# Accumulators of one PSUM bank in place of halves of a bank pair: a hybrid HGRN2 / Mamba-2 layer on one core

## The chip, the core and the metric

The kernel runs on one core of a Trainium2 chip, as one program. A core has TensorE (PE, matmuls), VectorE (DVE), ScalarE (ACT), GpSimd (POOL) and DMA queues, which SyncE (SP) issues here. Matmuls write into PSUM, of which the kernel uses eight banks of 512 float32 a partition; DVE and ACT read it. Each engine works off its own queue in order and waits on semaphores for the others. The metric is the time of one execution in microseconds on the device.

## The reference, cut to what matters

One inference step of one layer over T = 1048 tokens: 16 meta tokens, 1024 of a prompt, 8 single-token samples. Everything is float32.

```
h += 0.5 * SwiGLU_1(rmsnorm(h))                      D = 1024, hidden 2816
u  = rmsnorm(h) @ w_in                               q, f, i, g | z | x, B, C | dt
HGRN2, 4 heads of 128:  S_t = diag(f_t) S_{t-1} + k_t v_t^T,  o_t = S_t^T q_t,  k = 1 - f
        o = rmsnorm per head(o) * silu(g)
Mamba-2, 8 heads of 64: causal conv(4) + SiLU on x, B, C
        h_t = exp(dt_t A) h_{t-1} + dt_t x_t B_t^T,  y_t = h_t C_t + D x_t
        y = grouped rmsnorm(y * silu(z))
h += concat(o, y) @ w_out
h += 0.5 * SwiGLU_2(rmsnorm(h));  final rmsnorm of the outputs
```

The last states of both recurrences and of the convolution are outputs too.

## The kernel before

**Matmuls.** A float32 product is made of three matmuls on operands split into a high part (rounded by a copy on ACT) and a low part (a subtraction on DVE): `mm3`, lines 143 (high x high), 144 (high x low) and 145 (low x high). A *unit* is one accumulator's chain of such triples. Its result is read out of PSUM by an *evacuation* on ACT or DVE.

**Tokens.** The FFNs and out_proj work on quarters of Q = 262 tokens, two of them (c = 0, 1, or a half) at a time; the mixer's projections on chunks of 350, 350 and 348.

**PSUM.** Two pools share the eight banks: `mis`, four tiles of one bank for transposes, norms and scans (`psm()`), and `acc`, two tiles of two banks each, for the accumulators. `psum2()` hands out a whole tile, `psum()` the first half of a new tile and, at the next call, its second half. A tile's place comes free when all that was done with the tile is done.

**FFN** (`ffn`, line 691; hand-ordered). Both FFNs use products of a seven-multiplication scheme, numbered p. In `pair`, the gate and up products of one block of 128 hidden columns, p runs over 1, 6, 2, 5, 7, 3, 4; products 2, 3 and 4 add onto the accumulators of 1, 5 and 7. Except in the first pair of each FFN a unit pair (c = 0 and c = 1) shares one `psum2()` tile, which one instruction then reads whole. In the first pair (`first1`, `first2`) the operands are still being made (lines 281 to 298: scaling and high parts on ACT, sums and low parts on DVE), and each c has its own `psum()`; the accumulator of p = 7 and 4 is a `psm()`. There the copy of p = 1 is line 451, the reads of p = 6, 5, 3 are lines 453, 458 and 462. `down` runs p over 1, 5, 6, 7, 3, 4, 2; each p has four column groups j of 2 x 33 matmuls. The first six products use `psum2()`, the last (p = 2) one `psum()` per c and j: four units with c = 0, then four with c = 1. Line 647 is the evacuation (multiply by 0.5 and add to h) on DVE; lines 618 and 623 split the weights, 557 and 561 the hidden operand. What follows an FFN (`after1`: the next norm, lines 200 to 211, and the mixer's operand, lines 247 to 250; `after3`: the final norm and the stores) is hung between the steps of the last product. `Steps` holds the order: `before(i, fn)` puts work ahead of step i, and inside `manual_schedule` PE, DVE, ACT and SP keep that order.

**Mixer** (not ordered by hand: the tile library's planner plays the program through at build and fixes each engine's order from it). `proj` makes 24 matmuls of 350 columns for each chunk into a `psum()`; evacuations are on ACT: line 990 (x, B, C), 1308 (raw q or f), 1299 (v), 1289 (q), 1293 and 1294 (f), 1302 (g), 1246 (z). Between them stand `ssm_scan` (lines 1091 to 1158) and, for each of four heads, `hgrn_scan` (lines 1337 to 1505, among them the level products 1398 and 1407 that wait for DVE's line 1422), all in `mis` tiles. `K.weights` loads and splits weights (lines 137 and 138).

**out_proj** (planned too): four calls of 16 units of 12 matmuls, for half 0 and half 1 of the tokens and two halves of the contraction; each unit has a `psum()`, and line 1529 on DVE adds it to h. Behind half 0 the second FFN's `first2` begins on ACT and DVE.

**The end.** `LastFinal` normalizes the last three token tiles: `second` transposes into one `psum2()` and one `psm()` (line 1579) and ACT sums squares (line 1582); `third` does the last block.

## Time and profile before

| | us |
|---|---|
| median of 3 runs | 2083.57 (2081.5 to 2094.95) |
| profiled execution, its own time | 2081.47 |
| its span, first to last instruction | 2079.8 |
| PE busy | 1970.9 |
| DVE busy | 1474.5 |
| ACT busy | 825.2 |

The profile is of one execution. Times in it count from the span's start. In a row of the timeline stand start, duration, engine, line of the kernel, operation, output <- input and in brackets how long the engine stood before it and what ended that. A row of the waits gives who waited for whom, the sum, the number of times and the longest. Matmuls overlap: a duration of 0.28 us belongs to one every 0.12.

### The profile page before, as it was taken

The page shows a single profiled execution, that of the slowest core. Times are in us where ns is not written, and L with a number is a line of the kernel's source. Part 1 is how long each engine was busy: PE and PEld are TensorE (multiplying, and loading weights), DVE is VectorE, ACT ScalarE, POOL GpSimd, SP SyncE. Part 2 cuts the span into 40 slices and gives each one's busy share as a digit, 9 for nine tenths or more (in the row PEclk, how much of TensorE's full clock was granted, in tenths as well). Part 3 has the DMA queues.
Part 4 walks back from the last instruction along what each step waited for, and adds up shares of the span by engine and source line. Part 5 has one row for each costly group of instructions (what it writes and reads, how often), then busy time and mean ns, then how long its engine had stood idle before and what let it go on. Part 6 is the DMA issues. An engine that isn't in the chain of part 4 may idle for free.

```text
span 2079.8 us, 40798 instructions
## 1 busy us (share of the span) xinstructions
PE 1970.9 (95%) x16647; PEld 1915.7 (92%) x16647; DVE 1474.5 (71%) x2465; ACT 825.2 (40%) x1540; POOL 156.2 (8%) x197
## 2 busy tenths in 40 slices
PE   5899999999999899889989989989999999999996
PEld 5899999999999889888988878889999999999996
DVE  6777777777788676596455346777777777768973
ACT  7522222223534543574443344652222222354352
POOL 3000000000003210332011101210000000000000
PEclk8999999999999999999999999999999999999999
DMA  6223242335967621362022153222333242587851
GB/s 196 87 80 108 78 124 83 103 91 180 313 201 228 181 58 33 101 181 80 33 83 74 31 176 124 78 74 86 110 92 108 78 124 78 155 241 239 266 174 60
DMA packets 325042, 259.32 MB, mean 125 GB/s; under 512 B 17712, under 2 KB 301104, under 8 KB 324848
## 3 DMA queue, kind: packets, MB, share of 16 engines
q1 hardware_dynamic: 324616, 256.68, 40.7%
q8 instruction: 131, 2.15, 0.4%
q14 instruction: 55, 0.45, 0.1%
q0 software_dynamic: 224, 0.04, 0.0%
q10 hardware_dynamic: 16, 0.00, 0.0%
HBM read 191.26 MB, written 65.47 MB: 123 GB/s over the span
## 4 chain that ended last, share of the span: by engine, by line
PE 77%; DVE 10%; ACT 5%; DMA 4%; issue 3%; SPq 1%; POOL 0%; DVEq 0%; ACTq 0%; POOLq 0%
PE acc L143 24%; PE acc L145 23%; PE acc L144 23%; DMA r<-in_w_in_dram 1%; DVE u L561 1%; DVE ws L623 1%; DVE s L647 1%; DMA r<-in_w_ffn_up_dram 1%; DVE s L590 1%; DVE ws L138 1%; DMA r<-in_w_ffn_down_dram 1%; DVE u L287 0%; DVE ws L368 0%; PE mis L1449 0%; DVE r L613 0%
## 5 line engine op out<-in xcount | busy, mean ns | idle before, releaser
L143 PE MATMUL acc<-u,ws 128*128 128x262 f32 (+2 forms) x4504 | 1320.5, 294 | 39.3 <-ACT t L451 9.9
L145 PE MATMUL acc<-u,ws 128*128 128x262 f32 (+2 forms) x4504 | 1310.6, 291 | 0.6 <-DVE ws L368 0.5
L144 PE MATMUL acc<-u,ws 128*128 128x262 f32 (+2 forms) x4504 | 1309.1, 291 | 1.5 <-DVE u L561 1.5
L143 PEld LDWEIGHTS acc<-u,ws 128*128 128x128 f32 x4504 | 853.1, 190 | 54.4 <-ACT t L451 10.7
L144 PEld LDWEIGHTS acc<-u,ws 128*128 128x128 f32 x4504 | 857.8, 190 | 3.3 <-DVE u L561 1.9
L145 PEld LDWEIGHTS acc<-u,ws 128*128 128x128 f32 x4504 | 852.7, 189 | 2.6 <-DVE ws L368 1.1
L368 DVE TENSOR_TENSOR ws<-r,ws 128x512 fp32r<-128x512 f32 x308 | 211.7, 688 | 76.7 <-ACT ws L364 76.7
L364 ACT CAST ws<-r 128x512 fp32r<-128x512 f32 x308 | 173.2, 615 | 4.7 <-PE acc L145 3.1
L464 ACT ACTIVATE t<-t 128x524 f32<-128x524 f32 (+1 forms) x46 | 28.7, 623 | 305.4 <-DVE t L446 305.4
L360 DVE TENSOR_TENSOR r<-r,r 128x512 f32<-128x512 f32 x176 | 121.9, 695 | 11.7 <-DMA r<-in_w_ffn_up_dram 10.1
L204 POOL TENSOR_TENSOR t<-t,t 128x262 f32<-128x262 f32 x56 | 55.7, 1010 | 782.6 <-PE acc L145 626.6
L456 ACT ACTIVATE t<-t 128x524 f32<-128x524 f32 (+1 forms) x46 | 28.7, 624 | 215.3 <-DVE t L446 215.3
L561 DVE TENSOR_TENSOR u<-u,u 128x1048 fp32r<-128x1048 f32 (+1 forms) x84 | 97.8, 1166 | 8.8 <-ACT u L557 8.4
L138 DVE TENSOR_TENSOR ws<-r,ws 128x512 fp32r<-128x512 f32 x88 | 65.1, 753 | 48.0 <-ACT ws L137 47.9
L446 DVE TENSOR_TENSOR t<-t,u 128x524 f32<-128x524 f32 (+1 forms) x138 | 89.8, 679 | 3.3
L557 ACT CAST u<-u 128x1048 fp32r<-128x1048 f32 (+1 forms) x84 | 83.2, 993 | 1.3 <-DMA u<-hd 1.3
L647 DVE SCALAR_TENSOR_TENSOR s<-acc,s 128x524 f32<-128x524 f32 (+1 forms) x88 | 55.7, 648 | 38.1 <-PE acc L145 37.5
L137 ACT CAST ws<-r 128x512 fp32r<-128x512 f32 x88 | 53.9, 617 | 71.8 <-PE acc L145 42.4
L618 ACT CAST ws<-u 128x512 fp32r<-128x512 f32 (+1 forms) x72 | 42.1, 585 | 100.8 <-DVE u L613 95.0
L623 DVE TENSOR_TENSOR ws<-r,ws 128x512 fp32r<-128x512 f32 (+1 forms) x84 | 57.6, 697 | 32.6 <-ACT ws L618 32.5
L618 ACT CAST ws<-r 128x512 fp32r<-128x512 f32 (+1 forms) x84 | 47.4, 581 | 71.6 <-DVE r L613 41.0
L446 DVE TENSOR_TENSOR t<-acc,u 128x524 f32<-128x524 f32 (+1 forms) x46 | 31.3, 680 | 60.6 <-PE acc L145 60.6
(388 smaller groups left out, 1908.1 us busy)
## 6 DMA issues: line engine op xcount, KB each, us to landing
hd<-s SPq DMA_DIRECT2D x170, 262.0 KB
u<-hd SPq DMA_DIRECT2D x64, 524.0 KB
r<-in_w_ffn_down_dram SPq DMA_DIRECT2D x128, 256.0 KB
r<-in_w_ffn_gate_dram SPq DMA_DIRECT2D x88, 256.0 KB
r<-in_w_ffn_up_dram SPq DMA_DIRECT2D x88, 256.0 KB
r<-in_w_in_dram SPq DMA_DIRECT2D x56, 256.0 KB
r<-in_w_ffn_down_dram SPq DMA_DIRECT2D x64, 192.0 KB
u<-hd SPq DMA_DIRECT2D x28, 393.0 KB
```

The source lines that it names most:

```text
L138: self.nc.vector.tensor_sub(lo, src, hi.bitcast(F32))
L143: mm(ps, whi, xhi, start=first, stop=False, skip_group_check=more)
L144: mm(ps, whi, xlo, start=False, stop=False, skip_group_check=more)
L145: mm(ps, wlo, xhi, start=False, stop=last, skip_group_check=more)
L360: self.K.nc.vector.tensor_tensor(self.raw[p], self.raw[x], self.raw[y], op)
L364: self.K.nc.scalar.copy(self.w[p][:, : self.n * P], self.raw[p])
L368: self.K.nc.vector.tensor_sub(t[:, 512 : 512 + w], self.raw[p], t[:, :w].bitcast(F32))
L446: nc.vector.tensor_mul(t, t if src is None else src, spread.lanes(i, cs))
L557: K.nc.scalar.copy(hi, lo.bitcast(F32))
L561: K.nc.vector.tensor_sub(lo, lo.bitcast(F32), hi.bitcast(F32))
L618: nc.scalar.copy(w[p, j, g][:, : n * P], src)
L623: nc.vector.tensor_sub(t[:, 512 : 512 + n * P], box[0], t[:, : n * P].bitcast(F32))
```

## The change

Every accumulator that is read by itself becomes a tile of one bank. The pool `acc` now has either four tiles of one bank (`banks(1)`) or two tiles of two (`banks(2)`), on the same four banks. `banks(n)` closes the pool and opens the other. It is opened with four; at step 14 of each FFN, the first behind the first pair, it becomes two pairs; ahead of the last down product four again, which stay for the mixer, out_proj and the second FFN's first pair, or for the end. `psum()` no longer splits a pair, and `second` takes two tiles. No arithmetic, transfer or evacuation is changed.

```diff
-        self.acc = ent(tc.tile_pool(name="acc", bufs=2, space=PSUM))
         self.mis = ent(tc.tile_pool(name="mis", bufs=4, space=PSUM))
...
-        self.half = None
+        self.banks_ = ent(ExitStack())
+        self.banks(1)
+
+    def banks(self, n):
+
+        self.banks_.close()
+        self.acc = self.banks_.enter_context(self.tc.tile_pool(name="acc", bufs=4 // n, space=PSUM))
+        self.pairs = n == 2
...
     def psum2(self):
-        self.half = None
+        assert self.pairs
         return self.acc.tile([P, 2, 512], F32, tag="acc", name=self.uid("acc"))
 
     def psum(self):
-
-        if self.half is None:
-            t = self.psum2()
-            self.half = t
-            return t[:, 0]
-        t, self.half = self.half, None
-        return t[:, 1]
+        assert not self.pairs
+        return self.acc.tile([P, 512], F32, tag="acc", name=self.uid("acc"))
...
         else:
+            S.before(b, lambda: K.banks(1))
             then = after(S, h, b - 48 + 24, b + 12, b + 24)
...
         S = Steps()
+        S.before(14, lambda: K.banks(2))
         hidden = Hidden(K)
...
-        two = K.psum2()
-        self.ps = [two[:, 0], two[:, 1], K.psm()]
+        self.ps = [K.psum(), K.psum(), K.psm()]
```

## Prediction

> **What bounds the kernel now.** I read the page first: busy shares, then the chain that ended last, then the costliest groups.

> ```profile
> span 2079.8 us, 40798 instructions
> PE 1970.9 (95%) x16647; PEld 1915.7 (92%) x16647; DVE 1474.5 (71%) x2465; ACT 825.2 (40%) x1540; POOL 156.2 (8%) x197
> ...
> PE 77%; DVE 10%; ACT 5%; DMA 4%; issue 3%; SPq 1%; POOL 0%; DVEq 0%; ACTq 0%; POOLq 0%
> ```

> TensorE is busy for 1970.9 of 2079.8 us and carries 77% of the chain. The change moves no arithmetic, so all it can win is part of the 109 us in which TensorE stands. Next the busy time by stage, to see where it stands (stretch, its length, then each engine's busy time with its count):

> ```profile
> 690.00:745.00 55.00, 47.06 (x367) 44.99 (x366) 36.59 (x68) 26.85 (x55) 11.85 (x15) 1.00 0.58 174
> 745.00:1250.00 505.00, 468.05 (x4586) 430.23 (x4585) 302.52 (x621) 227.28 (x452) 81.58 (x86) 0.98 0.28 84
> 1250.00:1306.00 56.00, 53.14 (x388) 49.30 (x388) 36.10 (x66) 24.90 (x47) 9.52 (x12) 0.97 0.38 121
> 1306.00:1363.00 57.00, 51.60 (x392) 48.81 (x390) 46.65 (x73) 39.02 (x76) 13.97 (x14) 1.00 0.23 72
> 1394.00:1935.00 541.00, 539.78 (x4422) 539.11 (x4421) 410.62 (x630) 169.68 (x293) 0.00 (x0) 1.00 0.45 136
> 2015.00:2080.00 65.00, 47.72 (x381) 45.65 (x379) 28.89 (x76) 19.17 (x58) 0.00 (x0) 0.95 0.27 87
> ```

> Row 1394 to 1935 is the second FFN: bank pairs, nothing to win, 541 / 4422 = 0.122 us a matmul. That is the dense rate. The other rows are the stages that take single accumulators: the end of the first FFN, the mixer, the two halves of out_proj, the end of the second FFN. Out_proj's matmuls have the same 262 columns, but 56 / 388 = 0.144 us.

> Then the chain of waits of TensorE in those four stages, one after the other (total, times, longest):

> ```profile
> PE acc L143 <- DVE s L647: 5.5, 3, 2.5
> PE acc L143 <- ACT u L248: 1.8, 1, 1.8
> ...
> PE acc L143 <- ACT u L1308: 2.0, 1, 2.0
> PE acc L143 <- ACT u L1289: 1.1, 2, 0.8
> PE acc L143 <- ACT u L990: 0.9, 2, 0.7
> PE acc L143 <- ACT t L1246: 0.8, 1, 0.8
> PE acc L143 <- ACT u L1299: 0.7, 1, 0.7
> ...
> PE acc L143 <- DVE s L1529: 6.5, 12, 1.6
> ...
> PE acc L143 <- DVE s L647: 3.6, 3, 1.6
> PE acc L1579 <- ACT u L1582: 1.3, 2, 0.9
> ```

> In each row but the second, a matmul that opens an accumulator waits for the instruction that empties one. Which one? The timeline tells it, at the first two units of the last down product and in the first pair of the second FFN:

> ```profile
> 698.67 0.28 PE L143 MATMUL acc<-u,ws 128*128 128x262 f32 x1
> ...
> 702.54 0.28 PE L145 MATMUL acc<-u,ws 128*128 128x262 f32 x1
> ...
> 702.09 2.87 DVE L623 TENSOR_TENSOR u<-r,u 128x512 fp32r<-128x512 f32 x3
> ...
> 704.88 0.42 DVE L647 SCALAR_TENSOR_TENSOR s<-acc,s 128x262 f32<-128x262 f32 x1
> ...
> 705.35 0.39 PE L143 MATMUL acc<-u,ws 128*128 128x262 f32 x1 [2.53 <-DVE s L647]
> ...
> 1383.78 0.38 ACT L451 COPY t<-acc 128x262 f32<-128x262 f32 x1 [0.99 <-PE acc L145]
> ...
> 1384.21 0.39 PE L143 MATMUL acc<-u,ws 128*128 128x262 f32 x1 [0.47 <-ACT t L451]
> ```

> The unit begun at 698.67 has the tile's first half, the one at 705.35 the second half, in another bank. It starts 0.05 us after the read of the **first** half ends (704.88 + 0.42). At 1384.21 it is the same: p = 5 opens the second half right behind the copy out of p = 1's. So in the program the halves wait on each other, although no data passes between them. A slot, moreover, comes free only when both halves are read. DVE was late for reasons of its own (it splits weights from 702.09 on), and TensorE paid for it.

> **The change, part by part.** No arithmetic, DMA or evacuation is added or removed. A wait of length w costs more than the row says: between 702.54 and 705.35 lie 2.81 us where 0.12 would do, so 2.69 for a listed 2.53, and 0.1 more until the stream runs again. I add 0.25 a wait.

> *Added: pool switches.* The accumulator pool is closed and opened at step 14 of each FFN and ahead of the last down product. A pool laid on the memory of a closed one waits for every reader of the closed one. At step 14 the last readers are early:

> ```profile
> 68.42 0.43 DVE L462 TENSOR_TENSOR t<-acc,t 128x262 f32<-128x262 f32 x1 [0.26 <-PE acc L145]
> ...
> 71.13 0.28 PE L143 MATMUL acc<-u,ws 128*128 128x262 f32 x1
> ...
> 1392.16 0.42 DVE L462 TENSOR_TENSOR t<-acc,t 128x262 f32<-128x262 f32 x1
> ...
> 1394.52 0.28 PE L143 MATMUL acc<-u,ws 128*128 128x262 f32 x1
> ...
> 700.59 0.70 DVE L647 SCALAR_TENSOR_TENSOR s<-acc,s 128x524 f32<-128x524 f32 x1
> ...
> 2025.13 0.70 DVE L647 SCALAR_TENSOR_TENSOR s<-acc,s 128x524 f32<-128x524 f32 x1
> ...
> 2023.21 0.29 PE L143 MATMUL acc<-u,ws 128*128 128x262 f32 x1
> ...
> 2061.50 0.42 DVE L647 SCALAR_TENSOR_TENSOR s<-acc,s 128x262 f32<-128x262 f32 x1
> ```

> They end at 68.85 and 1392.58, 2.3 and 1.9 us before the pair's first matmul: products in the other pool (p = 4) cover it; cost 0. Ahead of the last product nothing covers it: the previous unit is read until 701.29 and 2025.83, TensorE could go on at 698.67 and 2023.21. Cost 2.7 us each, 5.4 together. Below, 0 if each tile waited for its own bank alone; I take 2.7, for the switch is of the whole pool. Behind the waiting matmul only TensorE queues; DVE, ACT and SP go on and work off their backlog.

> Does such a stop slow the clock (eighth column behind the length: granted clock)?

> ```profile
> 702.00:711.00 9.00, 6.47 (x53) 6.26 (x53) 5.19 (x8) 2.75 (x7) 2.94 (x4) 1.00 0.85 238
> 1377.50:1383.50 6.00, 5.66 (x24) 5.37 (x24) 5.88 (x10) 3.49 (x5) 0.00 (x0) 0.50 0.01 3
> 1377.74 0.58 PE L143 MATMUL acc<-u,ws 128*128 128x262 f32 x1 [6.37 <-DVE t L458]
> ```

> After a stop of 2.53 us the clock stays 1.00; after 6.37 us 24 matmuls take 6 us at 0.50. The new stops are 2.6 long, so none is charged; if they grew past some point between, each would cost some 24 x 0.12 = 3 us more. [...]

> *Out_proj, 1250 to 1363.* Against the dense rate the two rows are 56 - 388 x 0.122 = 8.7 and 57 - 392 x 0.122 = 9.2 us long. With four tiles a unit waits for the one four back, 3 x 12 x 0.122 = 4.4 us of cover against a read of 0.42. In the first half some 3 us are the ones-matmuls of the norm at 1250, which stay; I take 5. In the second half DVE is busy 46.65 of 57 us with the FFN's operands, in a fixed order, so it is late next; I take 4. Together 9, bounds 4 (only half of what is listed: 6.5 + 12 x 0.25 = 9.5) and 14.

> *First pair of the second FFN.* The 0.47 at 1384.21: 0.6. The 6.37 us ahead of 1377.74 is p = 3 waiting for the read of its own bank: it stays.

> *End of the first FFN into the mixer.* 5.5 + 3 x 0.25 = 6.2 less the switch of 2.7 is 3.5. Behind it the mixer's first units wait for their operand (1.8, L248) and for an ACT queue (0.9, L990), which more open units bridge in part; DVE, which makes that operand, is next. I take 5, bounds 0 and 8.

> *The rest of the mixer.* 2.0 + 1.1 + 0.8 + 0.7 + 6 x 0.25 = 6.1 listed. Here the order of TensorE is not written by hand but planned at build, and it will come out differently; I take 4, bounds below.

> *End of the second FFN.* 3.6 + 1.3 + 5 x 0.25 = 6.1 less 2.7; the tail's transposes still need the update of the residual at 2061.50. I take 2.7, bounds 1 and 4.

> **Sum:** 9 + 0.6 + 5 + 4 + 2.7 = 21.3. The profiled execution took 2081.47 us (span 2079.8 and 1.7 around it), 2.1 below the median of 2083.57: 2081.5 - 21.3 = **2060 us**.

> **Rivals.** *(1) The other engines take it back.* Where DVE or ACT are late anyway (mixer, second half of out_proj, operand of the mixer) TensorE only waits elsewhere. For it: DVE 82% busy in 1306 to 1363. Against it: 64% in 1250 to 1306, 44% in the tail. Left are the first half of out_proj 5, the tail 2.7, the pair 0.6: 2073.

> *(2) All is won.* Both out_proj rows to the dense rate less 3 (15), mixer 6 and as much again where scans fill better, ends 8 and 4, pair 1: 40 at most; half of the surplus over my sum, 9 us more, gives 2051.

> *(3) Slower: the mixer's new order.* Inside the four scans TensorE is kept busy by projections:

> ```profile
> sum 184.00, PE 92.71; mean PE 23.18
> ```

> That is the accumulator matmuls alone in the stretches 950:1000, 1036:1079, 1108:1153 and 1182:1228. If free accumulators let the plan run projections ahead of the scans, these stand bare: with half of the 92.7 us gone and the 17.3 us of the other terms won, 46 - 17 = 29 us slower, 2110. It decides from 17 / 92.7 = 18% on. Against it: the planner ranks by program order, in which the filling projections stand behind the scan, and weights are loaded one projection ahead.

> *(4) The change does not do what it says:* the first matmul waits for something else that ends at the same time; only the switches stay: 2081.5 + 5.4 = 2087.

> **How the numbers follow.** Forecast 0.55, with its own range 2052 to 2069; rival 1 0.22, rival 2 0.12, rival 3 0.06, rival 4 0.05. Leaving out rivals 3 and 4, the upper end of 1 and the lower of 2 gives 2047 to 2077. One per cent, about what a measurement here can tell from no change, is 2083.57 x 0.99 = 2062.7: six tenths of the forecast and rival 2 lie below it, 0.45; rival 3 above the other bound, 0.06; the rest, 0.49, within.

> **What would show it.** Right: no wait of L143 for L1529 or L647 inside the products; second units of the last product starting 0.12 us after the first end; out_proj at 0.125 to 0.13 us a matmul; one stop of 2.6 us, clock 1.00, ahead of each last product. Wrong: waits of the same size under other releasers (L1407, L1134, L298); fewer accumulator matmuls inside the scans; a stop at step 14, or a clock of 0.5 behind a switch.

## The result and the profile after

The changed kernel takes 2063.63 us, median of four runs (2059.18 to 2064.57), against 2085.03 (2081.5 to 2094.95) for the kernel before. The ratio, of the means of the runs here and below, is 0.9886, with a 95% interval of 0.9848 to 0.9923. The profiled execution took 2062.95 us. Line numbers are 1 higher up to the FFN and 3 higher behind it (143 is now 144, 647 is 648, 1529 is 1532).

The page of the changed kernel: span, busy times, the chain that ended last.

```profile
span 2061.2 us, 40795 instructions
...
PE 1966.5 (95%) x16647; PEld 1920.6 (93%) x16647; DVE 1472.6 (71%) x2465; ACT 827.5 (40%) x1540; POOL 156.5 (8%) x197
...
PE 72%; DVE 14%; DMA 6%; ACT 4%; issue 3%; SPq 1%; POOL 0%; ACTq 0%; DVEq 0%; POOLq 0%
```

TensorE's busy time moved by 4.4 us, the span by 18.6: 14.2 us of the gain are time in which TensorE stood. For the stages I cut both spans at the same instructions: the last read of a pair in the first FFN, the last copy of x, B, C, the first and the last output matmul of the SSM scan, the norm behind the last head, the first and last evacuation of out_proj, the last read of a pair in the second FFN, the end. Busy time by stage (stretch, length, PE, PEld, DVE, ACT, POOL, granted clock, DMA), first before, then changed:

```profile
700.60:849.70 149.10, 140.28 (x923) 131.20 (x922) 94.57 (x210) 59.38 (x123) 11.49 (x22) 1.00 0.23 67
...
866.00:946.80 80.80, 70.93 (x527) 63.28 (x528) 74.70 (x181) 55.82 (x121) 36.29 (x42) 0.98 0.56 166
946.80:1249.00 302.20, 278.03 (x3327) 256.32 (x3323) 151.73 (x272) 121.09 (x230) 42.28 (x34) 0.98 0.27 83
...
1254.90:1362.40 107.50, 99.80 (x760) 94.36 (x758) 77.92 (x128) 59.67 (x111) 23.50 (x26) 1.00 0.29 90
1362.40:2025.10 662.70, 653.66 (x5324) 651.79 (x5325) 506.39 (x785) 227.91 (x390) 1.51 (x2) 0.99 0.47 141
2025.10:2079.80 54.70, 37.62 (x298) 35.55 (x297) 20.24 (x58) 13.90 (x49) 0.00 (x0) 0.94 0.16 61
```

```profile
700.40:843.70 143.30, 141.79 (x938) 134.82 (x939) 94.05 (x210) 59.39 (x124) 12.27 (x22) 0.99 0.24 69
...
859.90:945.60 85.70, 74.37 (x538) 66.29 (x538) 75.47 (x183) 56.09 (x121) 33.09 (x42) 0.94 0.55 157
945.60:1245.20 299.60, 273.06 (x3300) 253.80 (x3297) 150.37 (x270) 120.73 (x228) 42.33 (x34) 0.98 0.28 84
...
1251.40:1347.30 95.90, 95.09 (x781) 94.55 (x780) 77.19 (x129) 60.59 (x113) 22.82 (x27) 1.00 0.31 97
1347.30:2008.10 660.80, 649.11 (x5290) 646.61 (x5288) 506.65 (x785) 227.69 (x389) 1.43 (x2) 0.99 0.47 142
2008.10:2061.20 53.10, 39.89 (x312) 38.66 (x312) 20.32 (x58) 13.69 (x49) 0.00 (x0) 0.89 0.17 64
```

The end of the first FFN with the mixer's first projections gave 5.8 us, out_proj 11.6 (it is dense now: 95.9 / 781 = 0.123 us a matmul), the second FFN 1.9, the tail 1.6. The SSM scan **lost** 4.9, and from the last copy of x, B, C to out_proj the mixer is 2.5 slower here (407.7 against 405.2; other profiles below scatter by 10). With 0.2 ahead of all this: 18.6.

TensorE's waits in the changed kernel, over the whole span (who waits for whom, sum, times, longest):

```profile
PE acc L144 <- DVE s L648: 5.2, 2, 2.6
PE acc L144 <- ACT ws L138: 4.8, 1, 4.8
```

The first row is the two pool switches and nothing else: the waits for line 1529 are gone from out_proj and those for line 647 from the inside of the products. The second row is new, one stop of 4.8 us for weights, in the SSM scan. At the first switch the timeline and the stretches around it read (in a stretch's row the granted clock is the third number from the end):

```profile
700.37 0.70 DVE L648 SCALAR_TENSOR_TENSOR s<-acc,s 128x524 f32<-128x524 f32 x1
...
701.21 0.56 PE L144 MATMUL acc<-u,ws 128*128 128x262 f32 x1 [2.60 <-DVE s L648]
```

```profile
697.74:701.16 3.42, 0.87 (x8) 0.66 (x6) 2.15 (x5) 2.36 (x5) 0.00 (x0) 1.00 0.76 204
701.16:704.58 3.42, 3.37 (x15) 3.40 (x16) 3.42 (x4) 2.12 (x5) 2.06 (x2) 0.50 0.61 161
875.24:878.65 3.41, 3.41 (x18) 2.77 (x19) 3.41 (x10) 2.35 (x5) 3.41 (x5) 0.50 0.37 116
2005.06:2008.47 3.41, 1.30 (x11) 1.09 (x9) 2.25 (x5) 2.03 (x4) 0.00 (x0) 1.00 0.84 231
2008.47:2011.88 3.41, 2.92 (x13) 2.95 (x14) 2.90 (x5) 2.15 (x5) 0.00 (x0) 0.50 0.16 43
```

The stop has the forecast length, but 3.41 us at half clock follow it, at both ends. Their starts lie on one grid: 875.24 - 701.16 is 51 x 3.413, 2008.47 - 701.16 is 383 x 3.413.

### The profile page after: what moved, and what is told of

It is laid out like the page before. It is cut to its first block, busy times and chain, and to the rows that moved or that the text cites. A ratio compares the mean times of both kernels' runs of the same rounds, so it can differ in the third digit from the quotient of the medians.

```text
span 2061.2 us, 40795 instructions
## 1 busy us (share of the span) xinstructions
PE 1966.5 (95%) x16647; PEld 1920.6 (93%) x16647; DVE 1472.6 (71%) x2465; ACT 827.5 (40%) x1540; POOL 156.5 (8%) x197
## 4 chain that ended last, share of the span: by engine, by line
PE 72%; DVE 14%; DMA 6%; ACT 4%; issue 3%; SPq 1%; POOL 0%; ACTq 0%; DVEq 0%; POOLq 0%
PE acc L144 22%; PE acc L145 22%; PE acc L146 22%; DVE u L562 2%; DMA r<-in_w_ffn_down_dram 2%; DVE ws L624 1%; DMA r<-in_w_in_dram 1%; DVE s L648 1%; DVE u L614 1%; DMA r<-in_w_ffn_up_dram 1%; ACT ws L619 1%; DMA u<-hd 1%; DVE u L299 1%; DVE s L591 1%; DVE r L614 1%
## 5 line engine op out<-in xcount | busy, mean ns | idle before, releaser
L145 PE MATMUL acc<-u,ws 128*128 128x262 f32 (+2 forms) x4504 | 1313.3, 292 | 1.5 <-DVE u L562 1.5
L145 PEld LDWEIGHTS acc<-u,ws 128*128 128x128 f32 x4504 | 860.5, 191 | 4.5 <-DVE u L562 1.9
L361 DVE TENSOR_TENSOR r<-r,r 128x512 f32<-128x512 f32 x176 | 121.2, 691 | 12.5 <-DMA r<-in_w_ffn_up_dram 11.0
L452 ACT COPY t<-acc 128x524 f32<-128x524 f32 (+1 forms) x46 | 26.6, 579 | 114.8 <-PE acc L146 114.8
```

The costliest lines, as they stand in the source:

```text
L145: mm(ps, whi, xlo, start=False, stop=False, skip_group_check=more)
L361: self.K.nc.vector.tensor_tensor(self.raw[p], self.raw[x], self.raw[y], op)
```

## The experiments

Three questions: does each stage's gain stand by itself, is it the wait between halves or the number of accumulators, and what became of the mixer's 4 us? All stretches of the profiled executions, in us, cut as above (10 is the third profile of the changed kernel, 11 the second of number 4):

| kernel | end of FFN 1 to last x copy | SSM scan | last x copy to out_proj | out_proj | tail |
|---|---|---|---|---|---|
| before, twice | 149.1, 149.2 | 80.8, 80.2 | 405.2, 404.7 | 107.5, 107.5 | 54.7, 54.6 |
| changed, three times | 143.3, 143.1, 143.0 | 85.7, 86.2, 85.6 | 407.7, 411.8, 411.3 | 95.9, 95.9, 95.9 | 53.1, 51.8, 53.4 |
| 1: halves in the mixer | 155.0 | 81.5 | 408.7 | 95.8 | 53.3 |
| 2: halves in out_proj | 143.3 | 85.9 | 407.1 | 107.7 | 53.2 |
| 3: halves at the ends | 149.5 | 85.6 | 407.5 | 95.9 | 54.6 |
| 4: no stop, twice | 140.2, 138.8 | 87.1, 87.0 | 408.7, 407.1 | 95.8, 95.8 | 49.0, 49.0 |
| 6: bank's own wait only | 142.7 | 86.3 | 401.6 | 95.9 | 51.8 |
| 7: out_proj on two banks | 140.5 | 85.3 | 411.1 | 98.6 | 49.0 |
| 8: halves in the scans | 138.5 | 87.0 | 409.9 | 95.6 | 49.0 |
| 12: z weights ahead | 138.7 | 84.7 | 403.4 | 95.8 | 50.1 |

**1 to 3: halves again in one stage.** In all three `psum()` can hand out halves as before, and a stage is put on pairs. The edits are shortened, and the comments are not in the code; 1 also goes back to four tiles ahead of out_proj, 2 keeps halves for the second FFN's first pair, and 3 also puts the final transposes back on a pair:

```diff
+    K.banks(2, "tile")        # 1: ahead of the mixer; four tiles again ahead of out_proj
     ssm_project(K, a, o)
...
+    K.banks(2, "tile")        # 2: ahead of out_proj
     out_proj(K, a, h, 0, opa, 0, mid=norm1)
...
-            S.before(b, lambda: K.banks(1))   # 3: and "tile" ahead of the mixer
```

Here "tile" means that a tile of the new pool waits for its own bank alone.

> The changed kernel, but in the mixer psum() hands out halves of a pair again (a switch to pairs behind the first FFN, back to four tiles ahead of out_proj; at these two switches each tile waits only for its own bank). Theory A (the mixer gained nothing: in the changed kernel the stretch from the last evacuation of the first FFN to the first of out_proj takes 514.4 us, before 513.3; the 22 us that its early projections run ahead are gone by the end of the SSM scan): the stretch comes out at 513 to 516 us and the time at the changed kernel's 2063.6, within 3 us. Theory B (my prediction's term, 4 us won in the mixer beside the 5 at its start, and something else was lost): the stretch is 4 us or more longer, 2068 or above.

> The changed kernel, but out_proj and the first pair of the second FFN take halves of pairs again. Theory A (the waits between halves are what out_proj lost, and the gain stands by itself): first to last evacuation of out_proj goes back from 95.9 us to 107.5, the first pair gives back 0.6 to 2.6, time 2063.6 + 12 to 14 = 2076 to 2078. Theory B (out_proj is faster because its operands come earlier or in a better order from the changed mixer): less than 5 us come back, 2068 or below.

> The changed kernel, but the last down products of both FFNs and the final transposes take halves of pairs as before, so no switch stands ahead of them; four tiles are opened ahead of the mixer and each waits only for its own bank. Theory A (the ends won what the traces show, 4.4 us at the first and 0.9 at the second): 2063.6 + 5 = 2069. Theory B (the stop of the switch, 2.9 us, and the 3.4 us at half clock behind it eat the whole gain at the ends): 2063.6 within 2 us.

Ratios to before: 0.9932 (0.9915 to 0.9949), 0.993 (0.9913 to 0.9948), 0.9927 (0.9908 to 0.9946), where the changed kernel has 0.9886, and 0.9889 and 0.9872 in later runs. (Before took 2089.6 to 2090.1 us beside these, on other chips, so ratios are compared.) Each gives back 0.004 to 0.006, that is 8.5 to 12.5 us.

Number 2 is theory A in out_proj: it is back at 107.7, with the old waits, and no other stage of the table is more than 0.6 us off the changed kernel's first profile; the second FFN behind it took 660.7, so the 1.9 us there are not the halves' doing, and the first pair gave nothing back. By the ratios 9 to 12 us came back where I had expected 12 to 14. (The stretch ahead of the table's first ends between 700.3 and 704.0 in the profiles, the same kernel's among them, so single profiles differ by some 3 us there.) Number 3 is theory A by its stretches: 149.5 and 54.6, the times of before, although the mixer's projections have four tiles. So the 5.8 us up to the last x copy come from the last product. These two stretches give 6.2 + 1.5 = 7.7 us, the ratios 8.5 to 11.5, where theory A had 5. Number 1 came out on theory B's side (743.27 to 1266.75, 523.5 us, where theory A had at most 516), but not for its reason. The waits of TensorE in its stretch 736 to 765, and the whole stretch:

```profile
PE acc L152 <- DVE s L656: 7.0, 1, 7.0
```

```profile
703.10:858.10 155.00, 146.40 (x938) 138.28 (x939) 94.66 (x210) 59.63 (x124) 11.72 (x22) 0.94 0.22 64
```

Its switch keeps the mixer's first units from starting between the last units of the FFN: a stop of 7.0 us, then a spell at half clock (0.94 over the stretch). Behind it the mixer took 408.7 with halves, 407.7 with four tiles. The experiment was confounded by its own switch; number 8 mends that.

**4: no stop ahead of the last product.** (`pool` stands for the call that opens a PSUM pool.)

```diff
-        self.acc = self.banks_.enter_context(self.tc.tile_pool(name="acc", bufs=4 // n, space=PSUM))
+        if n == 2:
+            self.acc = pool("acc", bufs=2, reuse_waits="tile")
+        else:
+            self.ab = [pool(f"acc{i}", bufs=2, reuse_waits="tile") for i in range(2)]
...
+        self.ab.reverse()
+        return self.ab[0].tile([P, 512], F32, tag="acc", name=self.uid("acc"))
```

> The changed kernel, but a tile of a newly opened accumulator pool waits only for the readers of its own bank, and the four tiles are two pools of two, taken in turn, so that the first unit of the last down product stands on a bank of the older pair, read 4 us earlier. Theory A (the stop ahead of the last product is the wait for all readers of the closed pool, and the half clock behind it follows from the stop): no stop of over 0.5 us there, clock 1.00, 2 x (2.8 + 1.7) = 9 us less than the changed kernel: 2054.6. Theory B (DVE is late by then and takes it back at the next units): the stop moves behind the second or third unit, 2060 to 2064.

> The version without the stop, again, beside the changed kernel on one chip. Theory A: two stops of 2.88 us are gone and with them half clock in most executions, 6 to 9 us less than the changed kernel of the same call. Theory B (the first comparison was luck of the clock): within 3 us of it.

Theory A, twice: ratio 0.9852 (0.9834 to 0.987), then 0.9844 (0.9827 to 0.9861) beside the changed kernel's 0.9872 (0.9852 to 0.9892) on the same chip; the medians there are 2057.32 and 2064.09, 6.8 us apart. The same two stretches in the second of its profiles:

```profile
700.40:839.20 138.80, 138.16 (x924) 131.29 (x923) 93.87 (x210) 59.37 (x124) 12.26 (x22) 1.00 0.24 72
2005.50:2054.50 49.00, 36.64 (x298) 35.37 (x297) 20.25 (x58) 13.71 (x49) 0.00 (x0) 0.93 0.19 69
```

Against the changed kernel's 143.3 and 53.1 they are 4.5 and 4.1 shorter. A stop of 2.60 us behind a matmul of 0.28 is 2.88 from start to start where 0.12 would do, 2.76 too many, and 3.41 us at half clock are 1.7: 4.5. This version beats both kernels.

**5 and 10: the changed kernel again.**

> The changed kernel once more, unaltered, for a second profile on another phase of the clock. Theory A (the clock is looked at in stretches of 3.41 us that run on by themselves; the next one is at half speed where TensorE stood for over some 55% of one): the stops ahead of the two last products are 2.60 us again, but each is followed by 3.4 us at half clock only where one stretch holds over 55% of it; other stops of 2 to 3 us change sides too, and the end of the stages moves by 1.7 us with each. Theory B (a stop of over 2.5 us halves the clock, wherever it falls): both stops are followed by half clock, as in the first profile. Time 2063.6 by the first chip, ratio to the kernel before 0.985 to 0.992.

> The changed kernel a third time, beside the version without the stop on one chip. Ratio to the kernel before 0.986 to 0.992; stops of 2.60 us ahead of both last products; SSM scan 85 to 87 us.

Ratios 0.9889 (0.9862 to 0.9917) and 0.9872. Theory A. Number 5's two stops are 2.59 and 2.60 us long; the stretches of its clock's grid around them:

```profile
700.68:704.10 3.42, 0.82 (x7) 0.81 (x7) 2.75 (x5) 3.19 (x7) 0.32 (x1) 1.00 0.69 176
704.10:707.50 3.40, 3.40 (x18) 3.40 (x17) 2.75 (x3) 1.29 (x3) 1.74 (x2) 0.50 0.63 175
2011.39:2014.81 3.42, 1.85 (x16) 1.64 (x14) 2.27 (x4) 1.83 (x4) 0.00 (x0) 1.00 0.69 194
2014.81:2018.22 3.41, 2.38 (x19) 2.41 (x20) 3.41 (x6) 2.69 (x6) 0.00 (x0) 1.00 0.36 96
2018.22:2021.63 3.41, 3.41 (x30) 3.41 (x29) 1.53 (x4) 0.00 (x0) 0.00 (x0) 1.00 0.00 0
```

The first stop falls into one grid stretch, TensorE is busy for 0.82 of it, and the next has 0.50. The second is cut in two, 1.85 and 2.38 are busy, and the clock stays. The first stop of experiment 1 is cut too (701.30 to 703.90):

```profile
702.11:705.52 3.41, 1.62 (x13) 1.65 (x14) 3.41 (x5) 3.31 (x8) 1.16 (x2) 1.00 0.81 219
705.52:708.94 3.42, 3.42 (x30) 3.42 (x29) 2.68 (x5) 0.69 (x2) 0.90 (x1) 1.00 0.48 115
```

In these stretches of dense matmuls 1.62 us busy were followed by 1.00, and 1.30 (at 2005.06 above) by 0.50.

**6: the bank's own wait only.** As number 4, but one pool of four with "tile".

> The changed kernel, but a tile of a newly opened pool waits only for the readers of its own bank; the four tiles stay one pool, so the first unit of the last product is placed on the bank of the pair that was read last. Theory A (the stop is the wait for the read of the bank that the first unit lands on): the stop stays at 2.6 us at both ends, and the time is the changed kernel's. Theory B (the rule of the pool is what costs): no stop, as with the two pools.

Theory A: one stop of 2.60 us (2.59 at the second end) stays at each end. What holds the first unit is the read of its own bank; the rule of the pool alone costs nothing here. The time was not the changed kernel's: the single run took 2056.16 us, mostly because its mixer took 401.6.

**7: two accumulators in out_proj** (on number 4):

```diff
-        self.ab.reverse()
+        if not self.only:       # set through out_proj
+            self.ab.reverse()
```

> The kernel with no stop ahead of the last products, but out_proj takes only two of the four single banks in turn: a unit waits for the read of the one two back. Theory A (out_proj lost to the wait of the second half for the read of the first, that is for the unit just before): out_proj takes at most 99 us from its first to its last evacuation (95.9 with four, 107.5 with halves), the time stays within 3 us of the kernel without the stop. Theory B (the number of free accumulators made the gain): 103 us or more, and 7 us or more lost.

Theory A by the stage. The ratio is 0.9868 (0.984 to 0.9895), some 3 to 5 us above number 4's two, which theory A had within 3; the intervals overlap. Waits of TensorE in out_proj, with two banks and then with halves (number 2):

```profile
PE acc L150 <- DVE s L1538: 2.2, 5, 0.8
```

```profile
PE acc L152 <- DVE s L1540: 8.5, 15, 1.4
```

Two banks that don't wait on each other take 98.6 us, four 95.9, four banks tied in pairs 107.5. Of the 11.6 us won, 8.9 are the tie and 2.7 the number. For the ends of the FFNs the two were not told apart.

**8: halves in the scans only** (on number 4, the switches behind the x, B, C projections and ahead of out_proj).

> The kernel with no stop ahead of the last products, but with a switch to pairs behind the projections of x, B, C, halves of pairs through the scans, and four tiles again from out_proj on. Theory A (the mixer behind those projections gains nothing from four single accumulators): from the last copy of x, B, C to the first evacuation of out_proj 405 to 409 us as in the kernels before and after, time within 3 us of the kernel without the stop. Theory B (it gains, and something else loses): 412 us or more, 4 us or more lost. The first experiment could not tell this, since its switch stood inside the start of the mixer.

409.9 us is just outside theory A's 405 to 409, and far enough from theory B's 412 only by the ratio: 0.9855 (0.9822 to 0.9889), the same as number 4 within the intervals. Behind the x projections no gain from single tiles shows.

**9: the kernel before again.**

> The kernel before, unaltered, for a second profile. With the changed order of the mixer the stretch from the last copy of x, B, C to the first evacuation of out_proj took 401.6 to 411.8 us in seven profiles of the same order (mean 408), with the order of before 405.2 in one. Theory A (the two orders cost the same, and one profile against one says nothing): this profile falls anywhere in 401 to 412. Theory B (the new order bares the SSM scan and costs some 3 to 5 us): 403 or less; the SSM scan itself, first to last output matmul, 81 us against the 85 to 87 of the new order in both cases.

404.7 and 80.2 us: theory A's by the mixer, theory B's by the scan. The scan's loss is real: 80.2, 80.8 and 81.5 us where the projections of x, B, C have halves (before twice, number 1), 84.7 to 87.1 in the eleven profiles where they have four tiles. The mixer as a whole is less so: 405.2 and 404.7 against a mean of 408.5 (401.6 to 411.8) over seven profiles (changed, 4, 5, 6, 7, 10, 11). Six of the seven lie above both, but number 1, with halves, took 408.7; whether the mixer lost is not shown.

What TensorE does in the scan can be seen, but not what lengthens it. Accumulator matmuls alone, in four parts of it, before and changed:

```profile
866.00:886.00 20.00, 6.62 (x41) 6.34 (x41) 0.00 (x0) 0.42 (x1) 0.91 0.75 230
886.00:906.00 20.00, 7.27 (x45) 6.76 (x44) 0.00 (x0) 1.24 (x3) 1.00 0.67 196
906.00:926.00 20.00, 10.36 (x60) 9.32 (x60) 0.00 (x0) 0.87 (x2) 1.00 0.73 217
926.00:946.80 20.80, 12.85 (x77) 11.92 (x75) 0.00 (x0) 1.38 (x3) 1.00 0.13 29
```

```profile
859.90:879.90 20.00, 9.04 (x55) 8.77 (x55) 0.00 (x0) 0.90 (x2) 0.91 0.79 234
879.90:899.90 20.00, 9.91 (x59) 9.39 (x59) 0.00 (x0) 1.35 (x3) 1.00 0.52 151
899.90:919.90 20.00, 6.10 (x28) 5.10 (x28) 0.00 (x0) 0.45 (x1) 0.83 0.86 241
919.90:945.60 25.70, 14.25 (x84) 13.45 (x84) 0.00 (x0) 1.40 (x3) 1.00 0.15 38
```

223 matmuls fill the scan before, 226 after: it isn't bared. But they come earlier (114 against 86 in the first 40 us), then TensorE reaches a z unit whose weights are not split yet and stands 4.83 us at 911.18, with scan matmuls queued behind it, and the clock drops (0.83 in that part). Neither is shown to be the cause. Number 8 has halves in its scan and no wait for weights there (its only wait for an accumulator or for weights from 855.1 to 942.1 follows), and its scan took 87.0 us, as long as number 4's, though TensorE stands 2.9 us for that accumulator instead; number 1 has 10.2 us at half clock in its scan, as much as the changed kernel, and took 81.5.

```profile
PE acc L156 <- ACT u L1314: 2.9, 1, 2.9
```

In these profiles the loss goes with four tiles in the projections ahead of the scan; by what path stays open.

**12: the weights of z ahead** (on number 4): they are loaded ahead of the first head's v projection.

> The version without the stop, but the weights of the first z projections (they stand behind the first head's v projection) are loaded ahead of that v projection instead of behind it. In all profiles of the new order TensorE stands 4 to 5 us inside the SSM scan at the first z unit, which waits for its weights, with scan matmuls queued behind it; in both profiles of before it does not. Theory A (running ahead into weights that are not there is what the SSM scan lost): no wait of over 1 us for the weights, the scan falls from 85 to 87 us to 80 to 82, 5 us or more less than the version without the stop: ratio 0.982. Theory B (the scan is bound by its own chain on DVE and the stop only fills time that is lost anyway): the scan stays above 84 us, ratio 0.983 to 0.987.

The edit did not do what it was for. Waits in its scan:

```profile
PE acc L150 <- ACT ws L144: 3.5, 1, 3.5
```

The stop is 3.5 us instead of 4.5, the scan 84.7; ratio 0.9846 (0.9825 to 0.9866), as number 4. By its numbers theory B, but the wait was not taken away, so whether the scan would be faster without it stays open.

## Why the prediction came out

**Total.** Forecast 21.3 us less, 2060 in 2047 to 2077. The medians differ by 21.4, the profiled executions by 18.5, and the median of 2063.63 lies within the forecast's own 2052 to 2069. The mechanism is shown: numbers 2 and 3 bring the old times of out_proj and of the two ends back, each in its own stage, and number 7 finds most of out_proj's gain in the tie between halves. The signs that I had named as right came: no wait for the evacuations inside the products, out_proj at 0.123 us a matmul, one stop of 2.6 us ahead of each last product. One that I had named as wrong came too, a clock of 0.5 behind a switch. The sizes are partly luck: terms that were too small stood beside one that brought nothing and a cost that was left out.

- **Out_proj, 9 us:** 11.6, in every run with four banks. The first half (5 forecast) gave 52.0 - 46.2 = 5.8, the second (4) 55.5 - 49.7 = 5.8. For the second I let DVE be late next since it is busy for 82% there; TensorE does not wait for it there any more. Rival 1 fell with that.
- **End of the first FFN into the mixer, 5 us:** 5.8, but from two mis-sized terms. Without the stop it is 149.1 - 138.8 = 10.3 (8.9 in number 4's first profile) where I summed 6.2 + 1.5; and the switch costs 4.5, not 2.7. What I left out is probably that the mixer's first units now stand between the FFN's last ones: from 718 to 743 us the changed kernel has 40 matmuls of 350 columns, before 16. No run takes that alone away.
- **End of the second FFN, 2.7 us:** 54.7 - 49.0 = 5.7 without the stop, near the 5.4 that I had before the switch; with it 1.6, 2.9 and 1.3 in three profiles.
- **Pool switches:** none at step 14, as forecast; 2.60 us at each last product, as forecast. But the lower bound, 0 if each tile waited for its own bank alone, was wrong: in number 6 it does, and the stop stays. The step that failed is the clock. I read one stop of 2.53 us with the clock at 1.00 and one of 6.37 with 0.50 as a limit on a stop's length. Of the twelve switch stops of 2.60 us in six profiles (changed, 1, 2, 5, 6, 10) nine were followed by half clock, which I had charged with nothing.
- **Rest of the mixer, 4 us:** nothing won, -2.5 in the profiles shown, inside the scatter. (The rows listed have five waits, not six, so they come to 5.9 and not 6.1.) The listed waits went, and a stop for weights and a longer scan came. Rival 3 named the planned order, but not in this way: the scan keeps its filling. What lengthened the scan stays open.
- **First pair, 0.6 us:** 1.9 by the rows, but number 2 has that stage on halves and 660.7 us as well, so it is not shown that the change did it.

Number 4, without the cost of the switches, comes to 0.985 x 2083.57 = 2052, near rival 2's 2051, but by chance: rival 2 had 15 us in out_proj and 12 in the mixer.

## What to carry to other kernels

Where two halves of one tile wait on each other in the program, give each accumulator that is read by itself a tile of its own, and look at the tie before the number: out_proj was faster on two separate banks (98.6 us) than on four tied in pairs (107.5). A pool that is reopened on the same banks cost a stop of 2.60 us at the first unit where that unit landed on a bank still to be read (changed, number 6), and none where the readers were done (step 14) or the bank was read earlier and was waited for alone (number 4). And where a planner sets the order, freer buffers can move work forward until something else, here the weights, is missing; look at the stages that you did not mean to change.

## What the runs showed of the hardware

Busy time by the profile does not sort all of them. Where TensorE stood for less than 23% the next stretch was at full clock 6887 times of 6916 (1062 of 1066 in before and changed), and in the other 29 the profile shows no standing at all. Both such stretches of the changed kernel hold 16 matmuls of one column. The first, with the stretch behind it, and these matmuls:

```profile
1062.98:1066.39 3.41, 3.41 (x27) 3.02 (x26) 1.37 (x4) 0.79 (x2) 0.10 (x1) 1.00 0.07 19
1066.39:1069.80 3.41, 3.41 (x9) 1.87 (x8) 0.04 (x1) 1.49 (x3) 0.00 (x0) 0.50 0.00 0
1064.00 1.93 PE L1489 MATMUL mis<-qs,r 128*128 128x1 f32 x16
```

An estimate for the stops of 2.60 us: in before and changed the longest that TensorE stood in a grid stretch with full clock behind it is 1.80 us (before, at 721.38, 1.61 busy). If the grid may leave no more than that of a stop in one stretch, parts x and 2.6 - x give x between 0.8 and 1.8, 1.0 of 3.41, three times in ten; it was three of twelve.
